# Filter taps in buffers of their own, and both halves' activations together, in a hybrid layer on one core

## The chip, the cores and the metric

The kernel runs on one core of a Trainium2 chip. Its engines work side by side, each on its own queue of instructions: TensorE (PE; PEld is its weight load), VectorE (DVE), ScalarE (ACT), GpSimd (POOL) and SyncE (SP), which here issues nearly all transfers. The metric is the time of one execution on the device, in microseconds (us): the median of several runs. A profile is one execution, recorded by the hardware; its span runs from the first to the last instruction.

## The reference: what is computed

One layer of an encoder on 256 tokens of width 4096, in float32:

```python
proj = rms_norm(x, norm_w) @ w_in                      # 4096 -> 14392 columns
# three groups of heads read their columns of proj:
xbc  = silu(causal_depthwise_conv(ssd_xbc, ssd_conv_w) + ssd_conv_b)   # width 4
qkv  = silu(causal_depthwise_conv(gdn_qkv, gdn_conv_w))                # width 4
o_fox = forgetting_attention(...)      # 8 heads;  rms_norm(o) * silu(fox_z)
y     = ssd_scan(...)                  # 24 heads; rms_norm((y + x*D) * silu(ssd_z))
o_gdn = gated_delta_rule(...)          # 12 heads; rms_norm(o) * silu(gdn_z)
return x + concat(o_fox, o_ssd, o_gdn) @ w_out         # 4096 -> 4096
```

The conv is `out[t] = sum over r of w[r] * in[t - 3 + r]`, channel by channel. The scans use matrices `exp(min(g[t] - g[s], 0))` of running sums of gates, masked to s <= t.

## The kernel before

**Projections.** Both projections are split: an operand is a rounded part (h) plus a rest (l), and three products of them are summed. For each k-tile of 128 rows, `split_w` makes `wh` on ScalarE (L203) and `wl` on VectorE (L204), with five buffers each, and `product` does six matmuls of 128x512, three for each half of the tokens (tb 0 and 1). A panel is 32 k-tiles, 512 columns. The weights stream through SP in tiles `wr` of two k-tiles (L226), four buffers. The product banks have three buffers, and a panel uses two.

**Units.** The 28 panels of the first projection are the units: gq, gk, gv, gz for each of three groups of the delta rule, then sB, sC, sx0 to 2, sz0 to 2 for the state-space part, then fq, fk, fv, fz twice. The first two run together with the norm of the input. When a panel ends, `take` empties its banks to `raw_<unit>` on ScalarE (L992; three raw buffers) and puts the unit's work into the queue `prep`. The output projection has eight more panels.

**Two queues of generators.** After each k-tile `drive` advances the generator at the head of `core` and then that at the head of `prep` by one tick; `yield n` lets n ticks pass. So the work of a unit is written out between the k-tiles of the next panels. `prep` holds the convs, norms and transposes; `core` holds the delta rule (`gdn_core`, of which `gdn_solve` is a blocked inverse in seven levels), its gated norm and output (`gdn_out`), the state-space groups and the attention.

**The planner.** The program text is then reordered by a planner that simulates the engines and takes, on each engine, the earliest-written instruction whose inputs it holds ready. Buffers with the same tag take turns, and a tile waits until an older one of its tag has been let go. `pin` puts an instruction behind the last instruction written before it on the same engine, and only that; it is used for the loads and the products of the convs and gates, since transfers land later than the planner's.

**A conv unit** (`conv_unit`, L446). The raw tile is stored to `past` in device memory (L452). The tap rows w[3], w[2], w[1], w[0] (and the bias, for the state-space units) are loaded spread over 128 partitions (L456), 256 KB each, into tiles of the tag "t2", which has eight buffers and also serves most tiles of the core's work. The raw tile is multiplied by w[3] (L461); the shifts by 1, 2 and 3 tokens are loaded back from `past` (L466; two buffers of tag "acc", so the third waits for the first), multiplied by their taps (L473) and added (L474), all on tiles of 128x1024. A SiLU per half follows (L485). In ticks after the unit's begin at 0: store and first tap at 1, first product and loads of two shifts at 5, their products at 10 and 12, load of the third shift at 12, its product at 16.

**Gates.** `gate_rows` loads rows of running sums, spread over the partitions, from device memory (L423). `decay` subtracts a column for each head (L430, VectorE) and takes the exp (L432, ScalarE, not pinned), a generator step per half. In `gdn_solve` the load stands 4 ticks ahead of the first half's use, and the second half's exp comes 6 ticks behind the first's; in a state-space group the two exps are 2 ticks apart. `silu_z` is a SiLU per half of a z unit, one tick apart (L727). Exp and SiLU lie in different function tables of ScalarE.

Of the kernel before, what the change touches and what calls it, by code (L numbers as in the profile page):

```python
# [15 lines left out]
AF = mybir.ActivationFunctionType  # L16
ALU = mybir.AluOpType
AX = mybir.AxisListType

P = 128  # L20
# [6 lines left out]
HG = 4  # L27
# [5 lines left out]
NDT, NGA, NFF, NBE = 24, 12, 8, 12  # L33
# [25 lines left out]
TAPS = 4  # L59
# [32 lines left out]
def tile_hybrid(ctx: ExitStack, tc: tile.TileContext, x, xT, w, wo, prm, cst, lev, cvw, out):  # L92
    nc = tc.nc
# [7 lines left out]
    dp = ctx.enter_context(tc.tile_pool(name="dram", bufs=1, space=bass.MemoryType.DRAM))  # L101
    ph = ctx.enter_context(tc.tile_pool(name="pshead", bufs=5, space=bass.MemoryType.PSUM))

    BUFS = {"raw": 3, "acc": 2, "keep": 4, "t2": 8, "vt": 2, "kt": 1, "qk": 2, "ot": 2}

    def r4(shape, dt=F32, name="r4", tag="acc"):
        return hp.tile(shape, dt, tag=tag, name=name, bufs=BUFS[tag])

    def t2(shape, dt=F32, name="t2", tag="t2"):
        return hp.tile(shape, dt, tag=tag, name=name, bufs=BUFS[tag])  # L110

# [9 lines left out]
    def v4(ap, n=4):  # L121
        return ap.rearrange("p (h c) -> p h c", h=n)
# [4 lines left out]
    def mid(ap, n):  # L127
        return ap.unsqueeze(1).broadcast_to([P, n, ap.shape[1]])


    pin = tc.keep_in_program_order
# [6 lines left out]
    U = cst_s[:, M_U:M_U + P]  # L138
# [208 lines left out]
    raw = {}  # L347
# [69 lines left out]

    gsum = dp.tile([2, NSP, P], F32, name="gsum")

    def gate_rows(tb, c0, n, name, tag="t2"):  # L420

        t = t2([P, n, P], name=name, tag=tag)
        pin(nc.sync.dma_start(out=t.rearrange("p a b -> p (a b)"),  # L423
                              in_=gsum[tb:tb + 1, c0:c0 + n, :].rearrange("o h l -> o (h l)").broadcast_to([P, n * P])))
        return t

    def decay(t, tb, c0, n):

        for i in range(n):
            pin(nc.vector.tensor_scalar(out=t[:, i, :], in0=t[:, i, :], scalar1=st["cs"][:, tb, c0 + i:c0 + i + 1],  # L430
                                        scalar2=0.0, op0=ALU.subtract, op1=ALU.min))
        nc.scalar.activation(t, t, AF.Exp)  # L432
        yield
        return t


    past = dp.tile([len(CONV), TAPS - 1 + T, 512], F32, name="past")
# [8 lines left out]
    def conv_unit(name, dst=None, bias=False):  # L446


        src = raw.pop(name)
        i = list(CONV).index(name)  # L450
        yield
        pin(nc.sync.dma_start(out=past[i, TAPS - 1:TAPS - 1 + T, :].rearrange("(b p) c -> p b c", b=2), in_=src))  # L452

        def taps(r):
            t = t2([P, 512], name="tap")
            pin(nc.sync.dma_start(out=t, in_=cvw[i, r:r + 1, :].broadcast_to([P, 512])))  # L456
            return mid(t, 2)

        w0 = taps(TAPS - 1)
        yield 4  # L460
        pin(nc.vector.tensor_tensor(out=src, in0=src, in1=w0, op=ALU.mult))  # L461

        def shifted(j):
            sh = r4([P, 2, 512], name="shift")
            r = TAPS - 1 - j
            pin(nc.sync.dma_start(out=sh, in_=past[i, r:r + T, :].rearrange("(b p) c -> p b c", b=2)))  # L466
            return sh, taps(r)

        got = [shifted(j) for j in (1, 2)]
        yield 5  # L470
        for j in range(1, TAPS):
            sh, wj = got[j - 1]
            pin(nc.vector.tensor_tensor(out=sh, in0=sh, in1=wj, op=ALU.mult))  # L473
            pin(nc.vector.tensor_tensor(out=src, in0=src, in1=sh, op=ALU.add))  # L474
            yield 2
            if j == 1:
                got.append(shifted(3))
            else:
                yield 2
        if bias:  # L480
            b = taps(TAPS)
            yield
            nc.vector.tensor_tensor(out=src, in0=src, in1=b, op=ALU.add)
        for tb in range(2):
            nc.scalar.activation(src[:, tb, :] if dst is None else dst[tb], src[:, tb, :], AF.Silu)  # L485
        yield
        return src

# [43 lines left out]
    gd = {}  # L532
# [37 lines left out]
        gd[g].update(ktail=kt, rs=rs)  # L570

    def gdn_v(g):
        vt = [t2([P, HG, P], name="vt", tag="vt") for _ in range(2)]
        yield from conv_unit(f"gv{g}", [v.rearrange("p h c -> p (h c)") for v in vt])
        gd[g]["vt"] = vt
        core.append(gdn_core(g))

    def mm4(name, lhs, rhs):
# [5 lines left out]
    def gdn_solve(g):  # L584

        qk, m32, m16 = [], [], []
        dr = [gate_rows(tb, NDT + HG * g, HG, "dmat") for tb in range(2)]
        yield 4
        for tb in range(2):
            kq = gd[g]["kq"][tb]  # L590
            dm = yield from decay(dr[tb], tb, NDT + HG * g, HG)
            ds = t2([P, HG, P], name="ds")
            nc.gpsimd.tensor_tensor(out=dm, in0=dm, in1=mid(U, HG), op=ALU.mult)
            nc.gpsimd.tensor_tensor(out=ds, in0=dm, in1=mid(ident, HG), op=ALU.subtract)
            yield
            q = t2([P, HG, P], name="qk", tag="qk")
            m = t2([P, HG, P], name="m32")
            for pr in range(2):
                ps = bank("kkps")
                pv = ps.rearrange("p (h a c) -> p h a c", h=2, a=2)  # L600
                for i in range(2):
                    h = 2 * pr + i
                    nc.tensor.matmul(ps[:, i * T:(i + 1) * T], kq[:, h, 0, :], kq[:, h, :, :], start=True, stop=True)  # L603
                yield
                for i in range(2):
                    h = 2 * pr + i
                    nc.vector.scalar_tensor_tensor(out=m[:, h, :], in0=pv[:, i, 0, :],
                                                   scalar=st["be"][:, tb, HG * g + h:HG * g + h + 1],
                                                   in1=ds[:, h, :], op0=ALU.mult, op1=ALU.mult)
                hs = slice(2 * pr, 2 * pr + 2)  # L610
                nc.vector.tensor_tensor(out=q[:, hs, :], in0=pv[:, :, 1, :], in1=dm[:, hs, :], op=ALU.mult)
                yield

            h16 = h1([P, HG, P], name="m16", tag="m16")
            nc.scalar.copy(h16, m)
            qk.append(q)
            m32.append(m)
            m16.append(h16)
            yield
# [3 lines left out]
        for n, b in enumerate(LEVELS):  # L623
# [4 lines left out]
            if n == 0:  # L628
                for tb in both:
                    ps = mm4("aps", lambda h: mb[tb][:, h, :], lambda h: idh)  # L630
# [5 lines left out]
            for tb in both:  # L636
                ps = mm4("yps", lambda h: mb[tb][:, h, :], lambda h: tn[tb][:, h, :])
# [15 lines left out]
        r, r16, v16, tf = [None] * 2, [None] * 2, [None] * 2, [None] * 2  # L653
# [69 lines left out]

    def silu_z(name):
        z = raw.pop(name)
        for tb in range(2):
            nc.scalar.activation(z[:, tb, :], z[:, tb, :], AF.Silu)  # L727
            yield
        return z

    def gdn_z(g):
# [8 lines left out]
    sd = {}  # L740
# [16 lines left out]

    def ssd_c(_):
        sd["C"], _ = yield from ssd_bc("sC")
        sd["cb"] = []  # L760
        for tb in range(2):
            ts = slice(tb * P, tb * P + P)
            ps = mm4("cbps", lambda g: sd["B"][:, g, ts], lambda g: sd["C"][:, g, ts])
            c = t2([P, 4, P], name="cb", tag="vt")
            nc.vector.tensor_tensor(out=c, in0=v4(ps), in1=mid(U, 4), op=ALU.mult)
            sd["cb"].append(c)
            yield
        sd["xt"] = [r4([P, 2, 512], name=f"xtok{u}", tag="keep") for u in range(3)]

# [1 line left out]

    def ssd_x(u):
        xt = sd["xt"][u]
        yield from conv_unit(f"sx{u}", [xt[:, tb, :] for tb in range(2)], True)
        core.extend(ssd_group(g) for g in SSD_GROUPS[u])

    def pieces(g):
# [7 lines left out]
    def ssd_group(g):  # L785
        hh = slice(6 * g, 6 * g + 6)
        y_off = None
        for tb in range(2):
            xd = t2([P, 6, 64], name="xd", tag="qk")
            for u, a, n, o in pieces(g):  # L790
# [3 lines left out]
                                        op=ALU.mult)  # L794
            m = []
            dr = [gate_rows(tb, 6 * g + 3 * i, 3, "dmat") for i in range(2)]
            yield 4
            for i in range(2):
                dm = yield from decay(dr[i], tb, 6 * g + 3 * i, 3)
                nc.vector.tensor_tensor(out=dm, in0=dm, in1=mid(sd["cb"][tb][:, g, :], 3), op=ALU.mult)  # L800
                m.append(dm)
                yield
# [14 lines left out]
            if tb == 0:  # L817
                nc.gpsimd.tensor_tensor(out=xd, in0=xd, in1=bc(st["tail"][:, hh], 64), op=ALU.mult)
                yield 2
                ps = bank("stps")  # L820
# [5 lines left out]
                ps = bank("yops")  # L826
# [3 lines left out]
                                        in1=bc(st["gam"][:, hh], 64), op=ALU.mult)  # L830
# [75 lines left out]
    def fox_gates(g):  # L906


        c0 = NDT + NGA + HG * g
        e0 = gate_rows(0, c0, HG, "e0", "kt")  # L910
        e1m = gate_rows(1, c0, HG, "e1m", "vt")
        yield 4
        e0m = t2([P, HG, P], name="e0m", tag="vt")
        pin(nc.vector.tensor_tensor(out=e0m, in0=e0, in1=mid(st["mneg"], HG), op=ALU.add))
        pin(nc.vector.tensor_tensor(out=e1m, in0=e1m, in1=mid(st["mneg"], HG), op=ALU.add))
        yield
        return e0, e0m, e1m
# [101 lines left out]
    for i in range(8):  # L1019
        cs = slice(i * 512, (i + 1) * 512)  # L1020
        ps = panel(wo[i].rearrange("p (j n) -> p j n", n=512), mix_split)
        for tb in range(2):
            ts = slice(tb * P, tb * P + P)
            xr = t2([P, 512], name="xres")
            nc.scalar.dma_start(out=xr, in_=x[ts, cs])
            n = 2 if i == 7 and tb == 1 else 1
# [56 lines left out]
```

## Time and profile before

| what | value |
|---|---|
| time, median of 3 runs | 1742.17 us (1741.36 to 1742.31) |
| the profiled execution | 1739.72 us, span 1737.9 us |
| busy share of the span | PE 99%, PEld 81%, DVE 67%, ACT 54%, POOL 5% |
| table loads of ScalarE, 1.28 us each | 10 at L432 (exp), 7 at L727, 6 at L485 (SiLU), 3 at L937 |
| loads: taps, shifts, gate matrices | 61, 42, 22 |

Busy shares are of the whole span; stages differ. A PE that is busy may still wait a little inside a matmul, whose end is modelled. Idle time of another engine counts only where TensorE then waits for it.

### The profile page before, as it was taken

The page shows a single profiled execution, that of the slowest core. Times are in us where ns is not written, and L with a number is a line of the kernel's source. Part 1 is how long each engine was busy: PE and PEld are TensorE (multiplying, and loading weights), DVE is VectorE, ACT ScalarE, POOL GpSimd, SP SyncE. Part 2 cuts the span into 40 slices and gives each one's busy share as a digit, 9 for nine tenths or more (in the row PEclk, how much of TensorE's full clock was granted, in tenths as well). Part 3 has the DMA queues.
Part 4 walks back from the last instruction along what each step waited for, and adds up shares of the span by engine and source line. Part 5 has one row for each costly group of instructions (what it writes and reads, how often), then busy time and mean ns, then how long its engine had stood idle before and what let it go on. Part 6 is the DMA issues. An engine that isn't in the chain of part 4 may idle for free.

```text
span 1737.9 us, 24143 instructions
## 1 busy us (share of the span) xinstructions
PE 1715.7 (99%) x8165; PEld 1410.1 (81%) x8165; DVE 1162.0 (67%) x2121; ACT 933.0 (54%) x1635; POOL 89.1 (5%) x73
## 2 busy tenths in 40 slices
PE   9999999998999999999999999999999999999999
PEld 7888878786888778887788888888888888888887
DVE  7668777786676887768776665555755765555554
ACT  6665555445555464546555555556555754444443
POOL 0000020001000020000222100000000000000000
PEclk9999999999999999999999999999999999999999
DMA  8768876665665857667886666665666677777764
GB/s 292 225 216 286 266 233 204 220 200 173 212 224 154 277 163 224 205 199 264 262 274 196 183 186 185 191 202 172 184 194 183 180 243 216 218 217 217 206 205 139
DMA packets 119507, 368.86 MB, mean 212 GB/s; under 512 B 12629, under 2 KB 16045, under 8 KB 119383
## 3 DMA queue, kind: packets, MB, share of 16 engines
q1 hardware_dynamic: 114055, 358.15, 66.4%
q10 hardware_dynamic: 5328, 9.17, 1.5%
q8 instruction: 64, 1.05, 0.2%
q14 instruction: 60, 0.49, 0.1%
HBM read 355.61 MB, written 11.67 MB: 211 GB/s over the span
## 4 chain that ended last, share of the span: by engine, by line
PE 72%; DMA 2%; DVE 1%; issue 1%; ACT 1%; SPq 0%; DVEq 0%; ACTq 0%
PE proj L216 22%; PE proj L214 22%; PE proj L215 22%; DMA tap<-in_cvw 1%; PE yp L809 1%; DVE wl L204 0%; PE kkps L603 0%; PE mps L506 0%; PE zps L581 0%; PE yps L581 0%; PE zqs L581 0%; DMA dmat<-gsum 0%; PE cor L581 0%; ACT L432 0%; PE o L581 0%
## 5 line engine op out<-in xcount | busy, mean ns | idle before, releaser
L204 DVE TENSOR_TENSOR wl<-wr,wh 128x512 fp32r<-128x512 f32 x1152 | 799.0, 708 | 476.9 <-ACT wh L203 420.6
L203 ACT CAST wh<-wr 128x512 fp32r<-128x512 f32 x1152 | 704.8, 621 | 713.8 <-DVE wl L204 304.0
L214 PE MATMUL proj<-wh,xhl 128*128 128x512 f32 x1792 | 707.0, 395 | 9.0 <-ACT wh L203 6.0
L215 PE MATMUL proj<-wh,xhl 128*128 128x512 f32 x1792 | 702.9, 392 | 0.0
L216 PE MATMUL proj<-wl,xhl 128*128 128x512 f32 x1792 | 678.8, 396 | 6.3 <-DVE wl L204 6.0
L214 PEld LDWEIGHTS proj<-wh,xhl 128*128 128x128 f32 x1792 | 337.3, 188 | 81.0 <-ACT wh L203 8.4
L216 PEld LDWEIGHTS proj<-wl,xhl 128*128 128x128 f32 x1792 | 334.9, 188 | 82.2 <-DVE wl L204 14.8
L215 PEld LDWEIGHTS proj<-wh,xhl 128*128 128x128 f32 x1792 | 337.3, 188 | 69.1
L215 PE MATMUL proj<-wh,mhl 128*128 128x512 f32 x512 | 199.4, 390 | 0.0
L214 PE MATMUL proj<-wh,mhl 128*128 128x512 f32 x512 | 199.3, 390 | 0.0
L216 PE MATMUL proj<-wl,mhl 128*128 128x512 f32 x512 | 195.5, 390 | 0.0
L216 PEld LDWEIGHTS proj<-wl,mhl 128*128 128x128 f32 x512 | 96.2, 188 | 19.9
L214 PEld LDWEIGHTS proj<-wh,mhl 128*128 128x128 f32 x512 | 96.1, 188 | 19.9
L215 PEld LDWEIGHTS proj<-wh,mhl 128*128 128x128 f32 x512 | 96.2, 188 | 19.9
L473 DVE TENSOR_TENSOR shift<-shift,tap 128x1024 f32<-128x1024 f32 x42 | 51.3, 1221 | 20.5 <-DMA tap<-in_cvw 20.3
L648 DVE TENSOR_TENSOR tn<-tn,zps 128x512 f16<-128x512 f16 (+1 forms) x36 | 24.5, 682 | 3.5 <-PE zps L581 3.5
L649 DVE TENSOR_TENSOR tt<-tt,zqs 128x512 f16<-128x512 f16 (+1 forms) x36 | 24.5, 680 | 0.0
L793 POOL TENSOR_TENSOR xd<-xtok,spl 128x384 f32<-128x384 f32 (+2 forms) x12 | 16.7, 1398 | 127.5 <-ACT xtok L485 78.2
L430 DVE TENSOR_SCALAR dmat<-dmat,csum 128x128 f32<-128x128 f32 x72 | 16.4, 287 | 9.8 <-DMA dmat<-gsum 9.8
L657 POOL TENSOR_TENSOR res<-cst_s,tn 128x512 f32<-128x512 f32 x6 | 8.2, 1360 | 265.1 <-DVE tn L648 253.4
L639 ACT CAST y<-yps 128x512 f16<-128x512 f32 x36 | 19.3, 586 | 3.9 <-PE yps L581 3.8
L432 ACT ACTIVATE dmat<-dmat 128x384 f32<-128x384 f32 (+1 forms) x22 | 12.2, 554 | 14.5 <-DVE dmat L430 14.3
(302 smaller groups left out, 918.7 us busy)
## 6 DMA issues: line engine op xcount, KB each, us to landing
wr<-in_w SPq DMA_DIRECT2D x446, 512.0 KB, 3.8
wr<-in_wo SPq DMA_DIRECT2D x128, 512.0 KB, 3.6
shift<-past SPq DMA_DIRECT2D x42, 512.0 KB, 5.1
tap<-in_cvw SPq DMA_DIRECT2D x61, 256.0 KB, 6.4
xres<-in_x ACTq DMA_DIRECT2D x16, 256.0 KB, 4.9
xr<-in_xT SPq DMA_DIRECT2D x15, 257.0 KB, 4.9
out<-xres ACTq DMA_DIRECT2D x15, 256.0 KB, 4.2
dmat<-gsum SPq DMA_DIRECT2D x16, 192.0 KB, 6.5
```

Of the source, the lines that this page charges most:

```text
L203: a = nc.scalar.copy(wh, wr)
L204: b = nc.vector.tensor_tensor(out=wl, in0=wr, in1=wh.bitcast(F32), op=ALU.subtract)
L214: nc.tensor.matmul(ps[tb], h, wh, start=k == 0, stop=False)
L215: nc.tensor.matmul(ps[tb], lo, wh, start=False, stop=False)
L216: nc.tensor.matmul(ps[tb], h, wl, start=False, stop=k == KT - 1)
L430: pin(nc.vector.tensor_scalar(out=t[:, i, :], in0=t[:, i, :], scalar1=st["cs"][:, tb, c0 + i:c0 + i + 1], scalar2=0.0, op0=ALU.subtract, o ...
L473: pin(nc.vector.tensor_tensor(out=sh, in0=sh, in1=wj, op=ALU.mult))
L639: nc.scalar.copy(y[tb], v4(ps))
L648: nc.vector.tensor_tensor(out=tn2, in0=tn[tb], in1=v4(zp), op=ALU.subtract)
L649: nc.vector.tensor_tensor(out=tt2, in0=tt[tb], in1=v4(zq), op=ALU.subtract)
L793: nc.gpsimd.tensor_tensor(out=xd[:, o:o + n, :], in0=xv, in1=bc(st["spl"][:, tb, h0:h0 + n], 64), op=ALU.mult)
L809: nc.tensor.matmul(yp[:, h * 64:h * 64 + 64], m[h // 3][:, h % 3, :], xd[:, h, :], start=True, stop=True)
```

## The change

Each conv unit gets its taps from a tag of its own, "tap", with three buffers, and loads w[3], w[2], w[1] at once behind the store; w[0] is loaded a tick after the first product and the bias behind the third shift's load. In ticks: store and three taps at 1, loads of two shifts and first product at 7, w[0] at 8, the products at 13 and 15, load of the third shift at 14, its product at 20. `decay` keeps only the VectorE part; `exps` takes the exps of both tiles together, pinned. Gate matrices are loaded 6 ticks ahead. SiLUs cover both halves in one instruction, so the tiles behind them (v, the state-space cb, the fox masks) become one tile of both halves in one "vt" buffer instead of two.

```diff
-    BUFS = {"raw": 3, "acc": 2, "keep": 4, "t2": 8, "vt": 2, "kt": 1, "qk": 2, "ot": 2}
+    BUFS = {"raw": 3, "acc": 2, "keep": 4, "t2": 8, "vt": 1, "kt": 1, "qk": 2, "ot": 2, "tap": 3}
...
     def decay(t, tb, c0, n):
...
-        nc.scalar.activation(t, t, AF.Exp)
-        yield
-        return t
+
+    def exps(ts):
+        for t in ts:
+            pin(nc.scalar.activation(t, t, AF.Exp))
...
     def conv_unit(name, dst=None, bias=False):
...
         def taps(r):
-            t = t2([P, 512], name="tap")
+            t = t2([P, 512], name="tap", tag="tap")
             pin(nc.sync.dma_start(out=t, in_=cvw[i, r:r + 1, :].broadcast_to([P, 512])))
             return mid(t, 2)
 
-        w0 = taps(TAPS - 1)
-        yield 4
-        pin(nc.vector.tensor_tensor(out=src, in0=src, in1=w0, op=ALU.mult))
+        tap = [taps(r) for r in range(TAPS - 1, 0, -1)]
+        yield 6
...
-            return sh, taps(r)
+            return sh
 
         got = [shifted(j) for j in (1, 2)]
+        pin(nc.vector.tensor_tensor(out=src, in0=src, in1=tap[0], op=ALU.mult))
+        yield
+        tap.append(taps(0))
         yield 5
         for j in range(1, TAPS):
-            sh, wj = got[j - 1]
-            pin(nc.vector.tensor_tensor(out=sh, in0=sh, in1=wj, op=ALU.mult))
-            pin(nc.vector.tensor_tensor(out=src, in0=src, in1=sh, op=ALU.add))
-            yield 2
+            pin(nc.vector.tensor_tensor(out=got[j - 1], in0=got[j - 1], in1=tap[j], op=ALU.mult))
+            pin(nc.vector.tensor_tensor(out=src, in0=src, in1=got[j - 1], op=ALU.add))
+            yield 1
             if j == 1:
                 got.append(shifted(3))
-            else:
-                yield 2
+                if bias:
+                    tap.append(taps(TAPS))
+            yield 1 if j == 1 else 4 if j == 2 else 1
         if bias:
-            b = taps(TAPS)
-            yield
-            nc.vector.tensor_tensor(out=src, in0=src, in1=b, op=ALU.add)
-        for tb in range(2):
-            nc.scalar.activation(src[:, tb, :] if dst is None else dst[tb], src[:, tb, :], AF.Silu)
+            nc.vector.tensor_tensor(out=src, in0=src, in1=tap[TAPS], op=ALU.add)
+            yield
+        nc.scalar.activation(src if dst is None else dst, src, AF.Silu)
         yield
...
     def gdn_solve(g):
...
         dr = [gate_rows(tb, NDT + HG * g, HG, "dmat") for tb in range(2)]
-        yield 4
+        yield 6
+        for tb in range(2):
+            decay(dr[tb], tb, NDT + HG * g, HG)
+            yield
+        yield
+        exps(dr)
+        yield
         for tb in range(2):
-            kq = gd[g]["kq"][tb]
-            dm = yield from decay(dr[tb], tb, NDT + HG * g, HG)
+            kq, dm = gd[g]["kq"][tb], dr[tb]
...
     def silu_z(name):
         z = raw.pop(name)
-        for tb in range(2):
-            nc.scalar.activation(z[:, tb, :], z[:, tb, :], AF.Silu)
-            yield
+        nc.scalar.activation(z, z, AF.Silu)
+        yield
         return z
...
     def ssd_group(g):
...
             dr = [gate_rows(tb, 6 * g + 3 * i, 3, "dmat") for i in range(2)]
-            yield 4
+            yield 6
             for i in range(2):
-                dm = yield from decay(dr[i], tb, 6 * g + 3 * i, 3)
+                decay(dr[i], tb, 6 * g + 3 * i, 3)
+            yield 2
+            exps(dr)
+            yield
+            for dm in dr:
                 nc.vector.tensor_tensor(out=dm, in0=dm, in1=mid(sd["cb"][tb][:, g, :], 3), op=ALU.mult)
```

## Rows read from the trace of the kernel before

**Rows 1.** page, part 1: engine, busy us (share of the span), instructions

```profile
PE 1715.7 (99%) x8165; PEld 1410.1 (81%) x8165; DVE 1162.0 (67%) x2121; ACT 933.0 (54%) x1635; POOL 89.1 (5%) x73
```

**Rows 2.** page, part 4: the chain that ended last, by line

```profile
PE proj L216 22%; PE proj L214 22%; PE proj L215 22%; DMA tap<-in_cvw 1%; PE yp L809 1%; DVE wl L204 0%; PE kkps L603 0%; PE mps L506 0%; PE zps L581 0%; PE yps L581 0%; PE zqs L581 0%; DMA dmat<-gsum 0%; PE cor L581 0%; ACT L432 0%; PE o L581 0%
```

**Rows 3.** busy time by stretch: length, PE, PEld, DVE, ACT, POOL, PEclk, DMA

```profile
383.00:412.00 29.00, 22.57 (x99) 18.06 (x98) 19.20 (x41) 18.84 (x28) 5.53 (x4) 0.97 0.56 182
...
412.00:455.00 43.00, 43.00 (x220) 35.04 (x219) 31.79 (x67) 21.75 (x38) 2.88 (x2) 0.98 0.58 180
...
564.00:622.00 58.00, 52.00 (x221) 39.55 (x220) 48.28 (x97) 32.92 (x55) 7.08 (x5) 1.00 0.74 242
...
763.00:792.00 29.00, 28.77 (x128) 23.08 (x127) 25.22 (x42) 14.12 (x25) 0.00 (x0) 1.00 0.93 306
...
822.00:860.00 38.00, 36.12 (x163) 28.05 (x161) 27.11 (x43) 15.88 (x27) 10.37 (x9) 1.00 0.80 256
```

**Rows 4.** PE's timeline from 399: start us, us, instruction, idle before

```profile
400.99 0.50 PE L214 MATMUL proj<-wh,xhl 128*128 128x512 f32 x1 [2.19 <-ACT raw_gz L992]
...
409.85 0.50 PE L214 MATMUL proj<-wh,xhl 128*128 128x512 f32 x1 [4.25 <-ACT wh L203]
```

**Rows 5.** ACT's timeline, 384 to 414

```profile
399.73 0.62 ACT L203 CAST wh<-wr 128x512 fp32r<-128x512 f32 x1 [4.58 <-DMA wr<-in_w]
...
401.54 1.28 ACT L432 ACT_TABLE_LOAD   x1
402.83 0.63 ACT L432 ACTIVATE dmat<-dmat 128x512 f32<-128x512 f32 x1
403.48 1.28 ACT L727 ACT_TABLE_LOAD   x1
...
409.20 0.60 ACT L203 CAST wh<-wr 128x512 fp32r<-128x512 f32 x1
```

**Rows 6.** by stretch, the instructions of L214 alone: length, PE (count), PEld

```profile
1509.00:1639.50 130.50, 74.70 (x193) 36.05 (x192) 1.00 0.72 214
```

**Rows 7.** ACT's groups of instructions: busy us, mean ns, idle before

```profile
L727 ACT ACTIVATE raw_gz<-raw_gz 128x512 f32<-128x512 f32 x6 | 3.6, 624 | 0.0
...
L875 ACT ACTIVATE fsq<-raw_fq 128x1024 f32<-128x1024 f32 x2 | 2.1, 1060 | 0.1
```

**Rows 8.** instructions that use a tap: idle before them, times, and what ended it

```profile
  DMA tap<-in_cvw: 38.6, 23
```

**Rows 9.** page, part 6: loads, KB each, us to landing

```profile
tap<-in_cvw SPq DMA_DIRECT2D x61, 256.0 KB, 6.4
...
dmat<-gsum SPq DMA_DIRECT2D x16, 192.0 KB, 6.5
```

**Rows 10.** SP's timeline around gk2's store and its taps

```profile
506.46 0.38 SPq L452 DMA_DIRECT2D past<-raw_gk  x1
...
560.79 0.92 SPq L456 DMA_DIRECT2D tap<-in_cvw  x2
```

**Rows 11.** DVE's timeline, 368 to 420

```profile
371.09 0.17 DVE L557 TENSOR_SCALAR ssqk<-ssqk 128x16 f32<-128x16 f32 x1
...
379.21 1.22 DVE L561 TENSOR_TENSOR raw_gk<-raw_gk,rsqk_y 128x1024 f32<-128x1024 f32 x1
...
382.10 0.67 DVE L494 TENSOR_REDUCE so<-sq 128x4 f32<-128x512 f32 x1
...
383.37 1.22 DVE L461 TENSOR_TENSOR raw_gv<-raw_gv,tap 128x1024 f32<-128x1024 f32 x1
...
415.01 2.18 DVE L526 SCALAR_TENSOR_TENSOR ot<-ot,rso_y,raw_gz 128x128 f32<-128x128 f32 x8
```

**Rows 12.** DVE's timeline, 564 to 622

```profile
566.03 1.23 DVE L461 TENSOR_TENSOR raw_gk<-raw_gk,tap 128x1024 f32<-128x1024 f32 x1 [2.16 <-DMA tap<-in_cvw]
...
606.98 2.19 DVE L526 SCALAR_TENSOR_TENSOR ot<-ot,rso_y,raw_gz 128x128 f32<-128x128 f32 x8
```

**Rows 13.** DVE's timeline, 826 to 856

```profile
837.64 1.27 DVE L430 TENSOR_SCALAR dmat<-dmat,csum 128x128 f32<-128x128 f32 x6 [3.61 <-DMA dmat<-gsum]
```

More of the change, by code (lines that the diff above doesn't have):

```diff
@@ L418, in tile_hybrid, with gate_rows @@
     gsum = dp.tile([2, NSP, P], F32, name="gsum")
-    def gate_rows(tb, c0, n, name, tag="t2"):
-        t = t2([P, n, P], name=name, tag=tag)
+    def gate_rows(tb, c0, n, name, tag="t2", into=None):
+        t = t2([P, n, P], name=name, tag=tag) if into is None else into
         pin(nc.sync.dma_start(out=t.rearrange("p a b -> p (a b)"),
@@ L572, in gdn_v @@
     def gdn_v(g):
-        vt = [t2([P, HG, P], name="vt", tag="vt") for _ in range(2)]
-        yield from conv_unit(f"gv{g}", [v.rearrange("p h c -> p (h c)") for v in vt])
-        gd[g]["vt"] = vt
+        vt = t2([P, 2, HG, P], name="vt", tag="vt")
+        yield from conv_unit(f"gv{g}", vt.rearrange("p t h c -> p t (h c)"))
+        gd[g]["vt"] = [vt[:, tb] for tb in range(2)]
         core.append(gdn_core(g))
@@ L759, in ssd_c @@
         sd["C"], _ = yield from ssd_bc("sC")
-        sd["cb"] = []
+        cb = t2([P, 2, 4, P], name="cb", tag="vt")
+        sd["cb"] = [cb[:, tb] for tb in range(2)]
         for tb in range(2):
@@ L763, in ssd_c @@
             ps = mm4("cbps", lambda g: sd["B"][:, g, ts], lambda g: sd["C"][:, g, ts])
-            c = t2([P, 4, P], name="cb", tag="vt")
-            nc.vector.tensor_tensor(out=c, in0=v4(ps), in1=mid(U, 4), op=ALU.mult)
-            sd["cb"].append(c)
+            nc.vector.tensor_tensor(out=cb[:, tb], in0=v4(ps), in1=mid(U, 4), op=ALU.mult)
             yield
@@ L773, in ssd_x @@
         xt = sd["xt"][u]
-        yield from conv_unit(f"sx{u}", [xt[:, tb, :] for tb in range(2)], True)
+        yield from conv_unit(f"sx{u}", xt, True)
         core.extend(ssd_group(g) for g in SSD_GROUPS[u])
@@ L910, in fox_gates @@
         e0 = gate_rows(0, c0, HG, "e0", "kt")
-        e1m = gate_rows(1, c0, HG, "e1m", "vt")
-        yield 4
-        e0m = t2([P, HG, P], name="e0m", tag="vt")
+        em = t2([P, 2, HG, P], name="em", tag="vt")
+        e0m, e1m = (em[:, tb] for tb in range(2))
+        gate_rows(1, c0, HG, "em", into=e1m)
+        yield 6
         pin(nc.vector.tensor_tensor(out=e0m, in0=e0, in1=mid(st["mneg"], HG), op=ALU.add))
```

## The prediction

> **What bounds the kernel now.** I read the busy line first: TensorE is busy in 99% of the span [rows 1]. The chain that ended last agrees: its largest parts are the three projection matmul lines, and the first entry that is no matmul is the load of a filter tap, 1% [rows 2]. So VectorE and ScalarE count only where they starve TensorE. Next the busy time by stretch, TensorE's column: it lacks 6.43 us of 29 between 383 and 412, 6.00 us of 58 between 564 and 622, 1.88 us of 38 between 822 and 860, but only 0.23 us between 763 and 792, where VectorE is busy for 25.22 of 29 us [rows 3]. The granted clock is 0.97 and 0.98 of full speed in the first stretch and the one behind it, after TensorE had stood still, and 1.00 in the others; 0.03 x 29 + 0.02 x 43 = 1.7 us of matmul time [rows 3]. These four gaps and the clock make 14.5 + 1.7 = 16.3 us (14.54 + 1.73); a change of filters and gates can hardly win more, since the matmuls stay as they are.
>
> In the first stretch two stalls hold the 6.4 us: 2.19 us waiting for ScalarE's raw_gz, the emptying of the product banks, and 4.25 us waiting for wh, ScalarE's rounded weights [rows 4]. ScalarE's timeline shows why: from 401.54 to 409.20 it does exp, SiLU, exp, SiLU, each with a table load of 1.28 us, and no wh [rows 5]. The halves of a gate matrix (core queue) and of a z unit (prep queue) take turns. The same four loads stand around 607 to 620.
>
> **The change, part by part.** One tick is one k-tile: 192 matmuls of one line, two per tick, in 130.5 us, hence 1.36 us [rows 6].
>
> *Exponentials and SiLUs together.* Followed through the yields, the pair of exps of gdn 1 and 2 now comes one tick after the z unit's single SiLU, so four loads become two. ScalarE's 7.66 us [rows 5] become 2 x 1.28 for loads, 2 x 0.63 for exps and 1.06 for a 1024-wide SiLU (the 1024-wide square takes 1060 ns, a 512-wide SiLU 624 [rows 7]): 4.88 us, 2.78 us less. Both times this lies on the path, because the five wh tiles that ScalarE is ahead last 5 x 1.36 = 6.8 us: a block of 4.9 us fits in, one of 7.7 doesn't. I take 2.8 us for each of the two stretches; bounds 0 (another wait takes over) and the whole 4.25.
>
> The Trainium skill (ScalarE: Activation LUTs, "What ACT_TABLE_LOAD costs") puts a switch at about 2.66 us, 1283 ns for the load and the rest a drain. By it the two switches saved would be 5.3 us per stretch, and the forecast some 5 us lower. The trace agrees with the load but shows no drain: the load at 401.54 ends where the exp at 402.83 begins, and the next load starts 0.02 us behind that exp [rows 5]. The sum uses the trace.
>
> *Taps in buffers of their own, at the unit's beginning.* In all, engines stood idle for 38.6 us before instructions that waited for a tap, 23 times [rows 8]; a tap lands after 6.4 us and a gate matrix after 6.5 [rows 9]. The old distances were 4 ticks (store to first product, third shift to its use, gate matrix to use), 5.4 us, less than either; the new ones are 6 ticks, 8.2 us. There is a worse wait behind it: taps shared eight buffers with the core's work. The store of gk2 is issued at 506.46 and its first taps at 560.79, 54 us later [rows 10], when the core has let go of buffers; then gk2 and gv2 run one upon the other. With their own buffers the taps go at once.
>
> But the conv's first product is pinned behind the last VectorE instruction traced before it. I counted the ticks in both versions. Before, that is the weight split for gv1, gk2 and sC. Afterwards it falls on tick 7 of the unit and lands, in just these three, behind the gated norm of the previous core (L526). So these three stay late, and the taps' gain is not a unit's worth. How late? In the trace the norm runs at 415.01, because its chain of 18 small operations starts after 382.10 and is interleaved with gv1's conv from 383.37 on [rows 11]. With that conv behind the norm the chain should run at the pace of gk1's 15, which went from 371.09 to 379.21 [rows 11], so in 10 us: norm at 392 plus some 5 us, because core 0 starts 6 ticks later, its pair of exps waits for both halves and its two halves then overlap. So gv1's conv starts at about 399 instead of 383, core 1's gates no longer wait for it, and gk2 begins where it did, near 566 against a norm that was at 606.98 [rows 12]. I therefore take half of the first stretch's other stall as won, 1.0 of 2.19 us (bounds 0 and 2.19), and 0.2 us in the second stretch on top of 2.8 (bounds 0 and 3.2): its waits for taps become waits for the third shift, but the 2.18 us of norms [rows 12] leave it.
>
> *State-space groups.* Here the program is on time, so the pins hold. Gate matrices that VectorE waited 3.61 us for at 837.64 [rows 13] get 2.7 us more; taps of sx1 and sx2 are there. Of the 1.88 us I take 1.4 (bounds 0 and 1.88). The groups become 6 ticks longer each, 24 in all, hidden since the z units gate what follows: the third z unit's gate cannot start before that unit's projection ends, in either version.
>
> *Clock.* Half of the 1.7 us, 0.9, if the shorter stall still lowers it once (bounds 0 and 1.7).
>
> *What is added.* One tap load per unit now waits on SP for the first product, a bias load for the second; v, cb and the fox masks become one buffer of both halves, free long before it is needed, since a core lasts about as long as its four units. No row shows the new pins; I bound them by 0 and by 4.8 us each (the mean of 6.43, 6.00 and 1.88 [rows 3], what a crowded stretch costs) and take 1.0 in all, near 0, because the stretch from 763 to 792 holds sC's and sx0's convs together at 0.23 us.
>
> Sum: 2.8 + 1.0 + 2.8 + 0.2 + 1.4 + 0.9 - 1.0 = 8.1 us. The profiled execution took 1739.72 us, 1.8 of it around the span of 1737.9; it goes to 1731.6. The runs' median, 1742.17, lies 2.45 us above it: 1734.
>
> **The rivals.**
> *All is won.* The taps no longer starve, the convs spread and every gap of rows 3 goes: 16.3 us, 1726; a few gaps below 1 us elsewhere could make it 1722. For it: even two convs at once, from 763 to 792, cost 0.23 us [rows 3]. Against it: the three pins.
> *Hidden anyway.* VectorE's 38.6 us of waits cost TensorE little already, since five wh tiles cover 6.8 us; only part of one table pair shows: 2 us, 1740. Against it: the 4.25 us stall is plainly ScalarE's.
> *The norm pin (slower).* The norms come no earlier than in the trace, 415.01 and 606.98 [rows 11, 12], so gv1 and gk2 start 32 and 41 us later than their 383.37 and 566.03, sC alike; each then falls together with the emptying of the banks and the next exps. Three stretches at 4.8 us are 14.3, less the 8.1: 1748. It decides from (8.1 + 3.5) / 3 = 3.9 us each. Against it: gk1's chain, 8 us with no conv between.
> *SP held (slower).* The tap load that waits for the first product holds the weight loads behind it. ScalarE stood 4.58 us for a weight tile before 399.73, and TensorE lost 2.19 [rows 4, 5]; if each of 14 conv units did so, 30.7 us less 8.1: 1765. It decides from 11.6 / 14 = 0.83 us per unit. Against it: the old third shift, too, had to wait on SP, for the buffer that the first shift gives back, and the crowded stretch lost 0.23 us with it [rows 3]. The Trainium skill (DMA: Bandwidth & Descriptors, "Anatomy of one DMA") says the same of where a wait sits: the issuing sequencer holds it, not the DMA engines. No run here shows it for the new load.
>
> **How the numbers follow.** Forecast 0.45 (own range 1728 to 1738), all won 0.20, hidden 0.18, norm pin 0.11, SP held 0.06. A measurement of this kernel tells 0.2%, 3.5 us, from no change. Faster: 0.64, from the first two less a sliver; same 0.19; slower 0.17. The range 1722 to 1746 leaves out SP held, half of the norm pin and little else.
>
> **What would show it.** Right: two table loads instead of four beside the takes of gz1 and gz2, and TensorE without the 4 us stall; taps issued right behind each store; no wait of VectorE for a tap; gates of the state-space groups without a wait. gv1, gk2 and sC starting right behind the norms, and these near 399 and 566, show the pin step; norms at 415 or later show its rival. Wrong: a first product that SP waits for while ScalarE waits for weights, or a stall at the emptying of the banks longer than 2.19 us.

## The result, and the profile after

The changed kernel takes 1716.53 us in the median (1715.95 to 1718.33, 4 runs), the kernel before 1741.76 us (1738.66 to 1742.31, 4 runs) beside it: a ratio of 0.986, 95% interval 0.9843 to 0.9878. It is faster, as forecast, but by about 25 us and not by 8; the time lies below the range. The profiled execution of after took 1718.33 us with a span of 1716.5: 21.4 us less than the profiled one of before.

Page of after, part 1 and part 4 (busy us; the chain by engine), which answer to [rows 1, 2]:

```profile
PE 1709.2 (100%) x8165; PEld 1410.8 (82%) x8165; DVE 1173.9 (68%) x2121; ACT 930.1 (54%) x1611; POOL 97.3 (6%) x73
...
PE 99%; DVE 0%; ACT 0%; issue 0%; DVEq 0%; ACTq 0%
```

The chain is now TensorE and nothing else. TensorE's idle time in the span was 1737.9 - 1715.7 = 22.2 us and is 1716.5 - 1709.2 = 7.3: 14.9 us less. Its "busy" time fell by 6.5 us more, with the same 8165 instructions, so there was waiting inside it. Part of it can be followed: a projection matmul's record lasts some 395 ns, but from its start to the next matmul's there are 227 ns where nothing waits, so the first 0.17 us of each stall counts as busy. Summed over all projection matmuls, what exceeds 227 ns from one start to the next is 47.8 us before and 27.1 after. So 20.7 of the 21.4 us are to be seen in the starts, and 16.2 of them in pairs that stand over 0.6 us too far apart (15 before, one after).

TensorE's largest waits in before (line, what it waited for, us in total, times, longest us):

```profile
PE proj L216 <- DVE wl L204: 6.0, 12, 1.1
PE proj L214 <- ACT wh L203: 6.0, 2, 4.2
PE proj L214 <- ACT raw_gz L992: 3.0, 2, 2.2
```

The same in after, all that are left:

```profile
PE proj L214 <- ACT raw_gz L1002: 1.9, 1, 1.9
PE warmps L154 <- DVE warm L151: 1.2, 1, 1.2
PE proj L214 <- ACT wh L203: 0.3, 1, 0.3
```

The stretches of [rows 3] in after, same columns (the work in them has moved by up to 21 us):

```profile
383.00:412.00 29.00, 29.00 (x138) 24.00 (x137) 22.18 (x51) 17.60 (x28) 6.61 (x4) 1.00 0.56 161
...
564.00:622.00 58.00, 55.88 (x247) 45.52 (x246) 50.74 (x92) 33.52 (x55) 11.86 (x5) 0.97 0.72 227
763.00:792.00 29.00, 29.00 (x134) 23.94 (x133) 25.34 (x49) 14.64 (x25) 0.00 (x0) 1.00 0.84 276
822.00:860.00 38.00, 38.00 (x180) 31.54 (x179) 31.93 (x54) 22.86 (x36) 9.38 (x8) 1.00 0.81 249
```

Only 2.1 us of idle TensorE are left in them, around the emptying for gz2, and the clock falls there instead of in the first stretch: 0.03 x 58 = 1.7 us, as much as before. ScalarE's timeline around the emptying for gz1, then for gz2:

```profile
393.40 1.07 ACT L733 ACTIVATE raw_gz<-raw_gz 128x1024 f32<-128x1024 f32 x1
...
397.64 1.28 ACT L436 ACT_TABLE_LOAD   x1
398.94 0.63 ACT L436 ACTIVATE dmat<-dmat 128x512 f32<-128x512 f32 x1
399.98 0.63 ACT L436 ACTIVATE dmat<-dmat 128x512 f32<-128x512 f32 x1
...
593.41 1.28 ACT L436 ACT_TABLE_LOAD   x1
594.71 0.64 ACT L436 ACTIVATE dmat<-dmat 128x512 f32<-128x512 f32 x1
595.76 0.63 ACT L436 ACTIVATE dmat<-dmat 128x512 f32<-128x512 f32 x1
597.32 1.25 ACT L1002 ACTIVATE raw_gz<-proj,xn_y 128x512 f32<-128x512 f32 x2
598.59 1.28 ACT L733 ACT_TABLE_LOAD   x1
```

Of the four table loads beside each emptying, one is left at gz1 [rows 5] and two at gz2. VectorE's waits for transfers of the convs and gates, against 38.6 us for taps [rows 8]:

```profile
DVE shift L476 <- DMA shift<-past: 8.3, 6, 2.4
...
DVE dmat L430 <- DMA dmat<-gsum: 2.0, 3, 0.8
...
DVE raw_sx L471 <- DMA tap<-in_cvw: 0.3, 1, 0.3
```

Waits for taps are all but gone. VectorE's timeline at the gated norms of cores 0 and 1, with the first products of gv1 and gk2 (compare [rows 11, 12]):

```profile
410.49 1.14 DVE L528 SCALAR_TENSOR_TENSOR ot<-ot,rso_y,raw_gz 128x128 f32<-128x128 f32 x4
411.54 1.22 DVE L471 TENSOR_TENSOR raw_gv<-raw_gv,tap 128x1024 f32<-128x1024 f32 x1
...
567.64 1.14 DVE L528 SCALAR_TENSOR_TENSOR ot<-ot,rso_y,raw_gz 128x128 f32<-128x128 f32 x4
568.70 1.22 DVE L471 TENSOR_TENSOR raw_gk<-raw_gk,tap 128x1024 f32<-128x1024 f32 x1
```

### The profile page after: what moved, and what is told of

Read it like the earlier page. It is cut to its first block, busy times and chain, and to the rows that moved or that the text cites. A ratio compares the mean times of both kernels' runs of the same rounds, so it can differ in the third digit from the quotient of the medians.

```text
span 1716.5 us, 24082 instructions
## 1 busy us (share of the span) xinstructions
PE 1709.2 (100%) x8165; PEld 1410.8 (82%) x8165; DVE 1173.9 (68%) x2121; ACT 930.1 (54%) x1611; POOL 97.3 (6%) x73
## 4 chain that ended last, share of the span: by engine, by line
PE 99%; DVE 0%; ACT 0%; issue 0%; DVEq 0%; ACTq 0%
PE proj L216 31%; PE proj L214 30%; PE proj L215 30%; PE kkps L610 1%; PE yp L818 1%; PE zps L583 0%; PE yps L583 0%; PE zqs L583 0%; PE gproj L243 0%; PE mps L508 0%; PE cor L583 0%; PE o L583 0%; PE vn L583 0%; PE atps L583 0%; PE warmps L154 0%; PE fps L900 0%
## 5 line engine op out<-in xcount | busy, mean ns | idle before, releaser
L214 PE MATMUL proj<-wh,xhl 128*128 128x512 f32 x1792 | 706.8, 395 | 2.1 <-ACT raw_gz L1002 1.9
L214 PEld LDWEIGHTS proj<-wh,xhl 128*128 128x128 f32 x1792 | 337.1, 188 | 72.2 <-ACT raw_gz L1002 2.3
L214 PE MATMUL proj<-wh,mhl 128*128 128x512 f32 x512 | 199.1, 390 | 0.0
L215 PEld LDWEIGHTS proj<-wh,mhl 128*128 128x128 f32 x512 | 96.1, 188 | 20.1
L214 PEld LDWEIGHTS proj<-wh,mhl 128*128 128x128 f32 x512 | 96.1, 188 | 19.9
L656 DVE TENSOR_TENSOR tt<-tt,zqs 128x512 f16<-128x512 f16 (+1 forms) x36 | 24.4, 679 | 0.0
L798 POOL TENSOR_TENSOR xd<-xtok,spl 128x384 f32<-128x384 f32 (+2 forms) x12 | 11.8, 994 | 129.9 <-ACT xtok L487 65.7
L600 POOL TENSOR_TENSOR dmat<-dmat,cst_s 128x512 f32<-128x512 f32 x6 | 10.1, 1694 | 154.2 <-ACT dmat L436 154.2
L173 DVE SCALAR_TENSOR_TENSOR xhl<-xr,xhl 128x256 fp32r<-128x256 f32 x32 | 15.3, 478 | 3.4 <-ACT xhl L172 3.4
```

The costliest lines, as they stand in the source:

```text
L173: pin(nc.vector.scalar_tensor_tensor(out=t[:, 1, :], in0=xr[:, jj, 0:T], scalar=sc, in1=t[:, 0, :].bitcast(F32), op0=ALU.mult, op1=ALU.sub ...
L214: nc.tensor.matmul(ps[tb], h, wh, start=k == 0, stop=False)
L215: nc.tensor.matmul(ps[tb], lo, wh, start=False, stop=False)
L656: nc.vector.tensor_tensor(out=tt2, in0=tt[tb], in1=v4(zq), op=ALU.subtract)
```

## The experiments

Twelve kernels ran, four together on one chip each time; the ratios are to the kernel before on the same chip, with 95% intervals.

**The parts one by one.** *e2_act*: exponentials and SiLUs together, with the conv's buffers and distances and the gates' distance of before.

```diff
-        for tb in range(2):
-            nc.scalar.activation(src[:, tb, :] if dst is None else dst[tb], src[:, tb, :], AF.Silu)
+        nc.scalar.activation(src if dst is None else dst, src, AF.Silu)
...
+        exps(dr)
```

> Before, with exps of both halves together and pinned and one SiLU for both halves, but the conv unit's taps, loads and distances and the gates' 4 ticks as before. Theory A: 5 to 8 us won, about 1735, the 38.6 us of waits for taps as before. Theory B: 15 us or more won, about 1726. If the parts add up, this run's gain and that of the conv alone make some 23 us, with 2 left for the gates' distance.

Measured: 1736.45 us, 0.9986 (0.9975 to 0.9997). Some 2.8 us, less than the 5 to 8 of theory A: the block of four loads does go (two are left at gz1 and two at gz2), and TensorE then waits for VectorE's wl for 9.8 us in 10 times, against 6.0 in 12 before. Its chain still shows the taps (start us, us, what):

```profile
394.30 5.29 DMA tap<-in_cvw
583.78 5.32 DMA tap<-in_cvw
596.18 6.34 DMA tap<-in_cvw
785.33 8.20 DMA tap<-in_cvw
```

*e1_conv*: the new conv unit whole (buffers, early loads, distances), SiLUs and exps per half.

```diff
+        tap = [taps(r) for r in range(TAPS - 1, 0, -1)]
+        yield 6
...
         for tb in range(2):
             nc.scalar.activation(src[:, tb, :] if dst is None else dst[tb], src[:, tb, :], AF.Silu)
```

> Before, with the whole new conv unit (taps in three buffers of their own, three loaded at the unit's beginning, distances 6, 6 and 6 ticks), but SiLUs and exps per half and gate matrices 4 ticks ahead as before. Theory A (the waits of VectorE for transfers are the larger part, and TensorE lost more to them than its idle column shows): 15 to 20 us of the 25 won, about 1724, no wait for a tap left, while the four table loads beside the take of gz1 stay. Theory B (the alternation of exp and SiLU is the larger part): at most 10 us won, about 1733.

Measured: 1719.46 us, 0.988 (0.9866 to 0.9895). The conv unit alone brings about 20 us of the 25, as theory A had it; 4.4 us of VectorE's waits for taps are left.

*e3_after_t2*: the changed kernel with its taps back in the shared tag.

```diff
-            t = t2([P, 512], name="tap", tag="tap")
+            t = t2([P, 512], name="tap")
```

> The changed kernel, but with the taps in the eight buffers shared with the core's work again; all loads and distances as changed. Theory A1 (the shared buffers held the taps back): most of the conv's gain is lost, 1728 to 1735, with first taps of gv1, gk2 and sC landing tens of us behind the store. Theory A2 (the distances do it): no more than 4 us lost, about 1719.

Measured: 1723.76 us, 0.9901 (0.9885 to 0.9918), between the two theories. Without own buffers most of the gain is still there; two of the edits must do in part the same thing. So the conv's edits were separated.

**Own buffers and early loads.** *e5_own*: the kernel before with own tap buffers alone, each tap loaded where it was.

```diff
-            t = t2([P, 512], name="tap")
+            t = t2([P, 512], name="tap", tag="tap")
```

> Before, with the taps in three buffers of their own and nothing else: each tap is still loaded beside its shift. Theory O (the buffers shared with the core held the taps back, and that made the convs pile up): 12 us or more won, about 1727, with gk2's and sC's taps no longer tens of us behind the store. Theory E (a tap loaded beside its shift lands after it, whichever buffer it has): at most 6 us won, about 1736, 30 us or more of VectorE's waits for taps left.

Measured: 1720.74 us, 0.9884 (0.9869 to 0.9899): more won than the 12 us of theory O, though VectorE still waits 28.9 us for taps, nearly what theory E named.

*e6_early_t2*: three taps loaded at the unit's beginning, in the shared tag.

```diff
-        w0 = taps(TAPS - 1)
+        tap = [taps(r) for r in range(TAPS - 1, 0, -1)]
         yield 4
...
         got = [shifted(j) for j in (1, 2)]
+        tap.append(taps(0))
```

> Before, with three taps loaded at the unit's beginning but in the eight shared buffers; old distances, exps, SiLUs and gates. Theory O: the taps are still held back, at most 8 us won, about 1734. Theory E: 12 to 16 us won, about 1726, as in the changed kernel with shared buffers (1723.76). If buffers and early loads need each other, this and the run with own buffers alone make together clearly less than the 24.4 us of both.

Measured: 1724.6 us, 0.991 (0.9893 to 0.9926): 17.0 us, a little more than theory E had. With the 20.8 us of own buffers that makes 37.8, well over the 24.4 of both, so the two don't need each other.

*e4_early*: both, with the old distances, and nothing else.

```diff
-            t = t2([P, 512], name="tap")
+            t = t2([P, 512], name="tap", tag="tap")
...
+        tap = [taps(r) for r in range(TAPS - 1, 0, -1)]
         yield 4
```

> Before, with taps in three buffers of their own and three of them loaded at the unit's beginning, but the old distances (4 from store to first product, 5 and 4 from a shift's load to its product) and the old exps, SiLUs and gates. Theory A1 (buffers and early loads): 10 to 15 us won, about 1729, with VectorE's waits moved from taps to shifts and small. Theory A2 (distances): under 5 us won, about 1738, VectorE now waiting 20 us or more for shifts that were hidden behind the taps' later landing.

Measured: 1714.86 us, 0.9854 (0.9839 to 0.9868): 24.4 us, where theory A1 had 10 to 15. SP's timelines show how the two single edits differ at gk2's store and taps. In e5_own the first tap is issued 0.5 us behind the store, the next 5.1 us behind that:

```profile
500.88 0.43 SPq L452 DMA_DIRECT2D past<-raw_gk  x1
501.36 0.46 SPq L456 DMA_DIRECT2D tap<-in_cvw  x1
...
506.46 0.79 SPq L456 DMA_DIRECT2D tap<-in_cvw  x1
```

In e6_early_t2 they are still held for 54.4 us, as before [rows 10], but then all four go at once:

```profile
498.71 0.38 SPq L452 DMA_DIRECT2D past<-raw_gk  x1
...
553.06 1.84 SPq L456 DMA_DIRECT2D tap<-in_cvw  x4
```

Own buffers take away that a unit begins late and falls upon the next; early loads, that it waits for one tap after another: 1.2% and 0.9% alone, 1.5% together. gk2's first product runs at 566.03 in before [rows 12], at 559.03 in e6_early_t2, at 508.22 in e5_own, and in e4_early, 5.8 us behind its store, at

```profile
503.09 1.23 DVE L461 TENSOR_TENSOR raw_gk<-raw_gk,tap 128x1024 f32<-128x1024 f32 x1 [1.08 <-DMA tap<-in_cvw]
```

The changed kernel itself does not get this: there it runs at 568.70, behind the norm, and what is gone is only the waiting. With both edits, TensorE's waits in e4_early are

```profile
PE warmps L154 <- DVE warm L151: 1.2, 1, 1.2
PE mps L507 <- DVE ot L527: 0.2, 1, 0.2
```

although VectorE still waits 13.3 us for taps, 5.0 of it at

```profile
DVE raw_sx L461 <- DMA tap<-in_cvw: 5.0, 3, 1.7
```

The sum of these waits does not tell the gain: 38.6 us before, 28.9 in e5_own, 23.2 in e6_early_t2, 13.3 in e4_early, for 0, 20.8, 17.0 and 24.4 us won.

**Turns or number.** *e9_t2_11*: the kernel before with eleven shared buffers, as many as the change has in both tags.

```diff
-    BUFS = {"raw": 3, "acc": 2, "keep": 4, "t2": 8, "vt": 2, "kt": 1, "qk": 2, "ot": 2}
+    BUFS = {"raw": 3, "acc": 2, "keep": 4, "t2": 11, "vt": 2, "kt": 1, "qk": 2, "ot": 2}
```

> The kernel before with eleven buffers of the tag t2 instead of eight; taps, activations and distances as before. Question: is it the number of buffers that held the taps, or that they take turns with the core's tiles? Theory A (turns): a tap waits for the tile eleven allocations back, which the core may still hold; three more buffers shift the hold from some units to others, and sC's or gk2's taps still start over 20 us behind their store: 1728 to 1738. Theory B (number): three more buffers do what three of their own did (1720.7 for own buffers alone): 1718 to 1724, no hold above 20 us in the delta rule's second and third group.

Measured: 1736.44 us, 0.9973 (0.9962 to 0.9984). gk2's taps:

```profile
506.61 0.38 SPq L452 DMA_DIRECT2D past<-raw_gk  x1
...
558.24 0.90 SPq L456 DMA_DIRECT2D tap<-in_cvw  x2
```

Still a hold of 51.6 us, as theory A had it: with eleven buffers in all, it matters that the taps take turns with the core's tiles. How many shared buffers would end the hold was not tried.

**The floor.** *e10_one_tap*: one tap tile, loaded once, in place of all 61 loads. It leaves out the other rows of coefficients, so its filters are not the layer's; products and adds are all there.

```diff
-            t = t2([P, 512], name="tap")
-            pin(nc.sync.dma_start(out=t, in_=cvw[i, r:r + 1, :].broadcast_to([P, 512])))
-            return mid(t, 2)
+            if "tap" not in st:
+                st["tap"] = cp.tile([P, 512], F32, name="tap")
+                pin(nc.sync.dma_start(out=st["tap"], in_=cvw[i, r:r + 1, :].broadcast_to([P, 512])))
+            return mid(st["tap"], 2)
```

> The kernel before with one tap tile, loaded once and used for every row of every unit, so 60 of the 61 tap loads are gone and the filters' coefficients are not the right ones; products, adds, shifts and activations as before. It shows what the taps' loads can cost at most. Theory A (waiting for taps was all that they cost): as good as own buffers with early loads, 1714.9: 1712 to 1717. Theory B (the 15.6 MB of loads, 256 KB each, also slow the weights): below 1711. Theory C (what remains of order decides): above 1718.

Measured: 1714.82 us, 0.9847 (0.9833 to 0.986), the same as e4_early; TensorE is busy for

```profile
PE 1706.8 (100%) x8165; PEld 1410.7 (82%) x8165; DVE 1170.7 (68%) x2121; ACT 928.7 (54%) x1629; POOL 97.3 (6%) x73
```

of a span of 1712.1. All that the taps cost was waiting; their traffic cost nothing that shows, and with early loads in own buffers nothing that shows is left of it to win.

**The rest of the change on top of it.** *e7_early_act*: e4_early with exponentials and SiLUs together, the gates at 4 ticks.

```diff
+        tap = [taps(r) for r in range(TAPS - 1, 0, -1)]
         yield 4
...
+        nc.scalar.activation(src if dst is None else dst, src, AF.Silu)
```

> Own buffers and early loads with the old conv distances (1714.86 alone), and exps and SiLUs of both halves together as in the changed kernel; gates 4 ticks ahead. Theory floor (after own buffers and early loads TensorE waits for nothing, so the activations have nothing left to win): 1713 to 1717. Theory additive (the 2.8 us of the activations alone come on top): 1711 to 1713.

Measured: 1720.56 us, 0.9884 (0.987 to 0.9899), 0.3% slower than e4_early, and slower than either theory had it. TensorE waits for wl again, for 3.2 us in 9 times.

*e8_early_act_gate6*: e7_early_act with gate matrices 6 ticks ahead, that is, the changed kernel but for the conv's distances.

```diff
-        yield 4
+        yield 6
```

> The changed kernel with the conv's old distances instead of the new ones, all else as changed. Theory cost (the longer distances themselves cost some 4 us, as between the conv alone, 1719.46, and own buffers with early loads, 1714.86): 1711 to 1714, below the changed kernel. Theory no cost (that difference came from the piling up of other work): 1716 to 1719, as the changed kernel.

Measured: 1722.22 us, 0.9891 (0.9877 to 0.9906): no clear difference to e7_early_act, and again slower than both theories. The changed kernel, which has the long distances too, lies 0.3% below it; but e1_conv, long distances without the activations together, lies 0.3% above e4_early. Neither edit has a sign of its own here.

*e11_early_again* and *e12_after_again*: e4_early and the changed kernel, side by side.

> The kernel before with own tap buffers and the first three taps loaded at the unit's beginning, nothing else, beside the changed kernel on the same chip. Theory A (activations together and longer distances bring nothing once the taps wait for nothing): 1714 to 1717, the same as the changed kernel or up to 3 us faster. Theory B (the other parts still help): 2 us or more slower than the changed kernel.

> The changed kernel once more, beside the one with early loads in own buffers alone. Theory A: 1716 to 1719, no faster than it. Theory B: 1714 or less, at least 2 us faster than it.

Measured: 1714.61 us, 0.9848 (0.9834 to 0.9861), and 1715.61 us, 0.9852 (0.9839 to 0.9866). No difference that can be told. The profiled execution of the second has a stall of 1.1 us at gz2 in place of 1.9, the clock stays at 1.00 in that stretch, and its span is 1713.7: 2.8 us between two executions of one kernel, 0.8 of it at that stall and 1.7 in the clock behind it.

When each panel's banks were emptied, against before in us (from the starts of the emptying in each trace):

| | gv0 | gz1 | gq2 | gv2 | gz2 | sx0 | fq0 |
|---|---|---|---|---|---|---|---|
| after | -2.1 | -8.7 | -12.4 | -13.4 | -20.0 | -17.5 | -21.5 |
| e2_act | +1.9 | -2.3 | -4.7 | -5.2 | -7.0 | -4.2 | -4.1 |
| e5_own | -2.2 | -5.0 | -8.2 | -7.6 | -15.9 | -15.5 | -20.6 |
| e6_early_t2 | -0.9 | -5.3 | -7.1 | -7.8 | -13.8 | -11.7 | -15.8 |
| e4_early | -1.8 | -6.5 | -9.8 | -10.8 | -20.0 | -20.1 | -25.0 |
| e9_t2_11 | +1.3 | -0.4 | +0.2 | +0.3 | -4.9 | -1.4 | -3.6 |

The largest step of the kernels that mend the taps is from gv2 to gz2, 6 to 9 us, where gk2's and gv2's convs had waited for their taps one upon the other; some of it is given back by sx0 in after and e6_early_t2.

## Why the prediction was wrong

Two steps failed: the price of the taps, put at 2.6 us where about 20 were won, and the ceiling of 16.3 us, which kept every forecast above the measured time. The direction came out as forecast, but 5.6 of the forecast's 8.1 us stood on the activations, which were not where the gain lay.

**The ceiling.** The prediction said that "a change of filters and gates can hardly win more" than 16.3 us. It added up four stretches; the span's whole idle was 22.2 us by the first line that it read [rows 1], and 6.5 us of waiting stood inside the busy time. The four stretches did give up 12.4 us of their 14.5; another 2.5 us of idle were won outside them. The rival "all is won" went in the right direction, but took its price from the same ceiling.

**The taps' terms: 1.0 + 0.2 us, and 1.4 with the gates.** Measured: own buffers alone 1.2% (20.8 us), early loads alone 0.9%. The prediction saw the 54 us hold and the missing distance. It held that mending them would win little, because three of the units stay late behind the norms anyway, and its rival "hidden anyway" held that five wh tiles cover VectorE's waits. Two rows of the kernel before tell otherwise. The first is the chain of waits of before in order of time, of whose taps only the share, 1%, was read [rows 2]:

```profile
571.34 6.25 DMA tap<-in_cvw
...
582.93 6.04 DMA tap<-in_cvw
...
596.18 6.87 DMA tap<-in_cvw
...
844.88 6.12 DMA tap<-in_cvw
```

That is 25.3 us on the chain that ended last, three of the four in 32 us. The second is VectorE's column in that stretch: 48.28 of 58 us busy [rows 3], and these waits beside it,

```profile
DVE shift L473 <- DMA tap<-in_cvw: 3.6, 2, 2.3
DVE raw_gv L461 <- DMA tap<-in_cvw: 2.5, 1, 2.5
DVE raw_gk L461 <- DMA tap<-in_cvw: 2.2, 1, 2.2
```

56.6 of 58 us together: VectorE was full there. Each wait for a tap delays the wl that stand behind it, and TensorE stood for wl six times between 579 and 616, 3.3 of its 6.0 us in that stretch; the other 2.6 it waited for ScalarE's wh and raw_gz. The first of the six stands behind the tap wait that ended at 577.68 (TensorE's timeline of before):

```profile
579.56 0.74 PE L216 MATMUL proj<-wl,xhl 128*128 128x512 f32 x2 [0.47 <-DVE wl L204]
...
605.90 0.73 PE L216 MATMUL proj<-wl,xhl 128*128 128x512 f32 x2 [1.07 <-DVE wl L204]
```

Elsewhere the same waits are free: e4_early has 13.3 us of them and the time of e10_one_tap, which has none. So the rival "hidden anyway" was wrong for that stretch and right for others.

**Activations: 2.8 + 2.8 us.** Alone they brought 2.8 in all, and on top of mended taps nothing, rather a loss (e7_early_act). The term for the second stretch was misread from the start. The four loads from 607 to 620 are no block like that of [rows 5] but two pairs, at 607.04 and 609.49 and at 615.48 and 618.58, with wh between them, and the second is for the SiLU of gv2's conv; TensorE waited 1.77 us for wh there, at 609.53. The middle two:

```profile
609.49 1.28 ACT L485 ACT_TABLE_LOAD   x1
...
615.48 1.28 ACT L432 ACT_TABLE_LOAD   x1
```

The rows show one reason why they bring nothing on top. ScalarE's function tables are loaded 29 times before (three of them in the first 120 us), 27 times in after, but 23 times in e4_early, which has the old activations: with the taps on time the core's exps no longer alternate with the z unit's SiLUs. In e4_early at gz1:

```profile
383.71 1.28 ACT L432 ACT_TABLE_LOAD   x1
385.00 0.63 ACT L432 ACTIVATE dmat<-dmat 128x512 f32<-128x512 f32 x1
...
392.72 0.64 ACT L432 ACTIVATE dmat<-dmat 128x512 f32<-128x512 f32 x1 [1.38 <-DVE dmat L430]
...
395.56 1.28 ACT L728 ACT_TABLE_LOAD   x1
```

The block of four loads was in part a consequence of the late convs. The Trainium skill (ScalarE: Activation LUTs, "What ACT_TABLE_LOAD costs") would have made the saving larger by a drain beside each load; no trace here shows one: in after the load at 598.59 starts 0.02 us behind the operation before it.

**Clock: 0.9 us.** Not won in the profiled execution of after, where it fell at gz2 in place of gz1; won in that of e12_after_again.

**Pins: order right, price wrong.** gv1 and gk2 do start right behind the norms, at 411.54 and 568.70, where 399 and 566 stood. The first norm is as late as the norm-pin rival had it in effect (410.49 against 415.01) and the second came 39 us earlier. No row shows a loss of TensorE by the first; the second stretch has the 1.9 us stall for raw_gz. What the prediction drew from it, that these units' taps bring little, was the mistake: gk2 began late as before, but without a wait for a tap.

**SP held** did not come: in after gk2's taps are issued 5.3 us behind its store, and TensorE has no wait for weights over 0.3 us.

**Open:** why the activations together cost 0.3% without the longer distances and these 0.3% without the activations. In e1_conv exps and SiLUs alternate again at gz1, with table loads at 395.10, 397.04 and 398.99, and TensorE waits 1.9 us for wh behind them; in e8_early_act_gate6 it waits 3.1 us for wl there, until 399.57. One candidate stands beside that wait: with the exps together, GpSimd's four masks of the gate matrices run in one block there, 393.38 to 398.97, where e4_early has two pairs of 2.7 us, and VectorE is slower beside GpSimd. In e8_early_act_gate6 a wl takes 0.69 us in the mean, and 1.25 us where GpSimd is busy for more than half of it. No run tried it, and the largest stalls of e7_early_act, at 251.1 and 872.8, have no such block before them. Why the order comes out so is not shown either: each edit shifts where the planner puts many instructions, and no kernel that changes the order alone was run.

## What to carry to other kernels

Read the chain in order of time, not by its shares. Here three transfers of 6 us stood on it one behind the other, in a stretch where busy time and waits fill an engine (56.6 of 58 us); without them that panel became 9 us shorter (e4_early, gv2 to gz2), while 13.3 us of the same waits elsewhere cost nothing. Take a ceiling from the whole span, and count that the first part of each stall (0.17 us here) hides in "busy". Loads that take turns in one pool with another queue's tiles are held by that queue, here with eleven buffers as with eight. Give them a pool of their own, and test the smallest such edit by itself: here own buffers with early loads were the whole gain.

## What the runs showed of the hardware

In the changed kernel a tap lands after 5.2 us in the median against 6.4 [rows 9], with the same sizes and count; that they crowd less would explain it, but no run tried it. In the profiled execution of after, TensorE's stall of 1.87 us that ended at 598.05 was followed by a granted clock of 0.66 until 602 and 0.92 until 606, 1.7 us lost; one of 1.1 us at the same place in e12_after_again was followed by 1.00. In before, 1.00 also followed the stall of 1.77 us that ended at 609.53, and 0.61 and 0.58 the one of 4.25 us that ended at 409.85.
